# Vector engine's order set in the source for a gated-attention and MLP kernel: additions, low parts, and bank evacuations by twos

## The chip, the core and the metric

The kernel runs on one core of one Trainium2 chip. The time is the device time of one execution in microseconds (us), the median of three runs.

## The reference

One layer of a streaming encoder on 256 tokens of width 2048, in float32: a gated linear attention, then a squared-ReLU MLP, each on a normalized input and added to the residual, and a last normalization.

```python
h = h + _gla_mixer(_rmsnorm(h, gla_norm[j]), ...)
h = h + _sq_relu_mlp(_rmsnorm(h, mlp_norm[i]), mlp_w_up[i], mlp_w_down[i])
return _rmsnorm(h, final_norm)

def _sq_relu_mlp(h, w_up, w_down):
    a = jax.nn.relu(h @ w_up)
    return (a * a) @ w_down
```

`w_up` is 2048 x 8192 and `w_down` 8192 x 2048. The change touches only the MLP.

## The kernel before

**High and low parts.** Every float32 matrix is multiplied as two parts: `hi`, a cast to the matmul's own format (ScalarE), and `lo`, the rest `x - hi` (the Vector engine). A product is three matmuls, hi x hi, hi x lo and lo x hi. So each 512 KB piece of weights goes through four stations: a load on SyncE's queue into one of six `raw` tiles, a cast on ScalarE into one of five `hi` slots, a subtraction on the Vector engine into one of five `lo` slots, and the matmuls on TensorE. `parts` (lines 117 and 118) does cast and subtraction for the down weights, `weights` (L137, L138) for the up weights. A matmul here has a 128 x 128 stationary operand and 256 moving columns.

**The MLP.** The hidden width of 8192 is cut into eight rounds (`ROUNDS`) of 1024. For each round the generator `up` multiplies the tokens with a part of `w_up`, in two halves (`q`) of eight steps; a step (`turned_steps`, L186) has 24 matmuls and sums into two banks of PSUM. At certain steps (`even`, in most rounds the fourth) the weights stand in the slot with a gap between their two halves (`gap=`), which shifts the second half by 64 bytes. At the end of a half, `forms` reads the two banks (`su`, L687), squares (ScalarE, L691), makes sums and differences of the blocks (L695) and their hi and lo (L702, L703); these `act` tiles are the stationary operands of the down product.

The generator `down` runs over `passes`: for each round four groups `g` of 512 output columns, and in each group four steps `kp`. Up and down steps alternate: the main loop takes one up step after each `yield` of `down`, and `up` begins 18 steps ahead. The groups are walked forward in odd and backward in even rounds, so that the group at the turn keeps its banks.

**Sums.** For most steps (`by_sums`) the down product of a 2 x 2 block is done with seven block products in place of eight, on sums of blocks. Such a step has two parts: 9 matmuls on three of the raw blocks (`lo<-raw` of 768 columns), and 12 matmuls on four sums of the raw blocks. The sums are made by three additions on the Vector engine (L754) in one of two `work` halves, then cast and subtracted like other weights (`hi<-work`, `lo<-work`). The other steps have 24 matmuls on the raw blocks. In a round of the middle, 11 steps have sums and 5 have none.

**Ends of a group.** A group sums into four banks (`b16`, `b32`, `b57`, `bx4`). After its last step two of them are added to `sums` tiles (L775; the first time copied on ScalarE, L773) and two to the residual `h` (`take`, L709). The list `free` hands banks on in order.

**Order.** The program is written down step by step, and a scheduler sets the order of each engine's queue out of it from data dependences and its own estimate of times. `tc.issue_after(ins)` puts what is issued inside it behind `ins` on the engine of `ins`. `last_hi` and `last_lo` hold the newest cast and subtraction. Small pieces of other work wait in the list `side` and are issued by `pump` during up steps.

Of the kernel before, what the change touches and what calls it, by code (L numbers as in the profile page):

```python
# [46 lines left out]
G = 1024  # L47
GT = 512
# [11 lines left out]
OFF = 48  # L60
EVEN = (5, 6)
MR = 2 * GT
# [6 lines left out]
def tile_gla_mlp(ctx, tc, x, xt, cols, w_vg, w_in, w_gate, w_out, w_up, w_down, final_norm, out):  # L69
    nc = tc.nc  # L70

    const = ctx.enter_context(tc.tile_pool(name="const", bufs=1))
    big = ctx.enter_context(tc.tile_pool(name="big", bufs=2))
# [8 lines left out]
    def psum_bank(i, name="acc"):  # L82
        return psum.tile([P, 512], F32, tag=f"b{i}", name=name)
# [10 lines left out]
    side = deque()  # L94
# [10 lines left out]
            side.popleft()()  # L105


    last_load, last_hi, last_lo = [None], [None], [None]

    def slots():  # L110
        return [wpool.tile([P, SLOT], F32R, tag=i, name=i) for i in ("hi", "lo")]

    def parts(raw, n, to, pieces=None):

        hi, lo = to
        for s in (slice(*p) for p in pieces or [(0, n)]):
            last_hi[0] = nc.scalar.copy(hi[:, s], raw[:, s])  # L117
            last_lo[0] = nc.vector.tensor_tensor(lo[:, s], raw[:, s], hi[:, s].bitcast(F32), op=ALU.subtract)  # L118
        return hi, lo
# [4 lines left out]
    def weights(src, n, pieces=None, room=None, gap=None):  # L124


        to = room or slots()
        raw = raw_tile()
        loads, pieces = pieces or ([(0, n)], [(0, n)])
        for s in (slice(*p) for p in loads):  # L130
            dst = raw[:, s]
            if len(src.shape) == 3:
                dst = dst.rearrange("p (i c) -> p i c", i=2)
                last_load[0] = nc.sync.dma_start(out=dst, in_=src)
                between = SLOT - OFF - 2 * GT if gap else 0
                to = [a[:, OFF - between : OFF + 2 * GT + between].rearrange("p (i c) -> p i c", i=2)[:, :, between:] for a in to]
                last_hi[0] = nc.scalar.copy(to[0], dst)  # L137
                last_lo[0] = nc.vector.tensor_tensor(to[1], dst, to[0].bitcast(F32), op=ALU.subtract)  # L138
# [34 lines left out]
    def turned_steps(row, w, c0, even, acc, flip=0):  # L173

        for kp in range(KT // 2):
            wh, wl = weights(w[2 * kp * P : 2 * (kp + 1) * P, c0 : c0 + GT].rearrange("(i p) c -> p i c", p=P), 2 * GT, gap=kp in even)
            for i in range(2):
                kt = 2 * kp + i
                ah, al = row(kt)
                for j in range(GT // P):  # L180
                    s = slice(j * P, (j + 1) * P)
                    k = j % 2 ^ flip
                    o = acc[j // 2][:, k * T : (k + 1) * T]
                    for n, (u, m) in enumerate(((wh, ah), (wh, al), (wl, ah))):

                        nc.tensor.matmul(  # L186
                            o, u[:, i, s], m, start=kt == 0 and n == 0 and j % 2 == 0,
                            stop=kt == KT - 1 and n == 2, skip_group_check=True,
                        )
                if kt < KT - 1:  # L190
                    pump()
            yield
# [160 lines left out]
    acc = natural(plain_x, rows(w_vg, 0, WMAX), WMAX, cuts, ahead=input_tile)  # L353
# [255 lines left out]
    acc = natural(row_o, rows(w_out, 0), G, HALF)  # L609
# [55 lines left out]
    free = deque([*acc_free, *aux_free])  # L665

    def up():
        for m in range(ROUNDS):
            for q in range(MR // GT):
                first = m == q == 0  # L670
                taken = [free.popleft() for _ in range(2)]
                acc = [psum_bank(i, "up") for i in taken]
                even = (6,) if first else (0,) if m == 0 else (3,) if q == 0 else ()
# [3 lines left out]
                act = big.tile([P, 4 * G + 64], F32R, tag="BC"[q], name="act")[:, OFF:-16]  # L677
                acts[m][q] = act = act.rearrange("p (b i f s) -> p b i f s", b=2, i=2, f=8)
                for b in range(2):
                    forms(m, 2 * q + b, acc[b], act[:, b])  # L680
# [27 lines left out]
    def take(bank, t, lo, n):  # L708
        nc.vector.tensor_tensor(h[:, t, lo : lo + n], bank, h[:, t, lo : lo + n], op=ALU.add)  # L709
# [4 lines left out]

    def down(passes):

        for n, (m, g) in enumerate(passes):
            if not n or passes[n - 1][1] != g:
                taken = [free.popleft() for _ in range(4)]
                b16, b32, b57, bx4 = (psum_bank(i) for i in taken)  # L720
            ends = n + 1 == len(passes) or passes[n + 1][1] != g
            for kp in range(KP):
                last = ends and kp == KP - 1
                at = lambda f: stationary(m, kp, f)

                def product(bank, o, a, w, c):

                    for i, (x, y) in enumerate(((0, 0), (0, 1), (1, 0))):
                        halves(bank[:, o], a[x], w[y][:, c], bank.name not in used, last and i == 2)
# [6 lines left out]
                if not by_sums(m, g, kp):  # L736
                    w = parts(raw, 2 * GT, slots())
# [3 lines left out]
                    yield  # L741
                    continue
                w = parts(raw, 2 * GT, slots(), [(T, 2 * GT)])
                block = lambda i: slice(i * T, (i + 1) * T)
                product(b16, left, at(A11), w, block(1))
                product(b32, right, at(A12), w, block(3))
                product(b32, left, at(S4), w, block(2))
                yield

                wk = work[:, n_sums[0] % 2]  # L750
                n_sums[0] += 1
                u = wk.rearrange("p (f s) -> p f s", f=4)
                raw = raw.rearrange("p (f s) -> p f s", f=4)
                add = lambda o, x, y: nc.vector.tensor_tensor(o, x, y, op=ALU.add)  # L754
# [5 lines left out]
                product(b57, left, at(S1), wu, block(0))  # L760
                product(b57, right, at(S3), wu, block(1))
                product(b16, right, at(S2), wu, block(2))
                product(bx4, right, at(A22), wu, block(3))
            if ends:

                e = sums[g]
                for dst, b in ((e[:, 1:3], b16), (None, b32), (e[:, 0::3], b57), (None, bx4)):
                    if dst is None:
                        take(b, 0 if b is b32 else 1, g * GT, GT)
                        continue  # L770
                    b = b.rearrange("p (f s) -> p f s", f=2)
                    if g not in begun:
                        nc.scalar.copy(dst, b)  # L773
                    else:
                        nc.vector.tensor_tensor(dst, b, dst, op=ALU.add)  # L775
                free.extend(taken)
                begun.add(g)
                if m == ROUNDS - 1 or m == ROUNDS - 2 and g > 1:
                    side.extend(combine(g))

    def combine(g):

# [117 lines left out]
```

## Time and profile before

| | before |
|---|---|
| median of 3 runs (lowest, highest) | 1106.53 us (1105.65, 1106.56) |
| the profiled execution | 1106.95 us, of which the span in the profile is 1104.9 us |
| TensorE clock granted | 0.998 of full speed over the span |
| load of a piece of `w_up`, `w_down`, issue to landing | 4.5 us, 4.0 us |
| read from and written to HBM | 206.92 MB, 2.10 MB |

PE is TensorE's matmuls, PEld its weight loads, DVE the Vector engine, ACT ScalarE, SP SyncE's queue. The end of a matmul is modelled at about 279 ns after its start, while the next one starts some 115 ns after it; so TensorE counts as busy over small gaps, and the number of matmuls in a stretch says more than its busy time. In rows of groups and waits, `<-` names what the engine stood idle for, in us.

### The profile page before, as it was taken

To read this page: it belongs to the slowest core of one execution; us is meant where nothing else is said; L and a number is where in the kernel's file an instruction comes from. 1 tells how busy PE (TensorE), PEld (TensorE's weight loads), DVE (VectorE), ACT (ScalarE), POOL (GpSimd) and SP (SyncE) were. 2 spreads that over 40 slices of the span, in tenths; PEclk is the share of its full clock that TensorE was granted. 3 is DMA by queue.
4 is the path that set the end of the run, shared out by engine and by line. 5 is a ranking of instruction groups with operands and counts; after the bars stand their busy time and mean duration, and the time that the engine had idled before them with its cause. 6 is when DMAs were issued, how large, how long until landed. Compare 5 with 4: busy or idle time off the path is not lost.

```text
span 1104.9 us, 22086 instructions
## 1 busy us (share of the span) xinstructions
PE 1083.0 (98%) x9202; PEld 1074.5 (97%) x9202; DVE 836.9 (76%) x1144; ACT 573.9 (52%) x723; POOL 12.8 (1%) x39
## 2 busy tenths in 40 slices
PE   9999999999999999999999999999999999999997
PEld 9999999999999999999999989999999999999997
DVE  5777655555646567788798888898888889888887
ACT  6775445454535454565554444644545545544553
POOL 0000000100000000000000000000000000000000
PEclk9999999999999999999999999999999999999999
DMA  9857665556565654665666646665556666575672
GB/s 341 319 155 214 204 193 149 156 159 187 190 189 175 191 175 151 187 211 175 191 190 185 198 154 203 186 212 169 184 177 194 192 184 194 170 226 172 201 238 77
DMA packets 94788, 210.45 MB, mean 190 GB/s; under 512 B 6704, under 2 KB 7600, under 8 KB 94560
## 3 DMA queue, kind: packets, MB, share of 16 engines
q1 hardware_dynamic: 93728, 206.99, 60.8%
q10 hardware_dynamic: 960, 2.05, 0.5%
q8 instruction: 72, 1.18, 0.4%
q14 instruction: 28, 0.23, 0.1%
HBM read 206.92 MB, written 2.10 MB: 189 GB/s over the span
## 4 chain that ended last, share of the span: by engine, by line
PE 86%; DVE 7%; issue 2%; ACT 2%; DMA 1%; SPq 0%; ACTq 0%; POOLq 0%; DVEq 0%; POOL 0%
PE acc L149 49%; PE up L186 28%; PE acc L186 6%; PE aux L186 2%; DVE lo L118 2%; ACT hi L117 1%; DVE lo L138 1%; DVE work L754 1%; DVE su L687 1%; DMA raw<-in_w_vg 1%; PE aux L149 1%; DMA zz<-in_xt 1%; PE aux L555 1%; PE aux L483 1%; DVE work L695 0%
## 5 line engine op out<-in xcount | busy, mean ns | idle before, releaser
L149 PE MATMUL acc<-hi,act 128*128 128x256 f32 x1864 | 336.7, 280 | 8.3 <-ACT hi L117 8.0
L118 DVE TENSOR_TENSOR lo<-raw,hi 128x768 fp32r<-128x768 f32 (+3 forms) x226 | 251.1, 1113 | 105.6 <-ACT hi L117 105.0
L149 PEld LDWEIGHTS acc<-hi,act 128*128 128x128 f32 x1864 | 277.7, 188 | 13.8 <-ACT hi L117 13.8
L117 ACT CAST hi<-raw 128x768 fp32r<-128x768 f32 (+3 forms) x226 | 216.3, 960 | 126.4 <-PE acc L149 103.0
L186 PE MATMUL up<-hl,hi 128*128 128x256 f32 x1024 | 281.7, 279 | 0.0
L186 PE MATMUL up<-hh,hi 128*128 128x256 f32 x1024 | 281.3, 279 | 0.0
L186 PE MATMUL up<-hh,lo 128*128 128x256 f32 x1024 | 273.1, 279 | 0.0
L149 PE MATMUL acc<-lo,act 128*128 128x256 f32 x932 | 221.3, 281 | 4.4 <-DVE lo L118 4.1
L138 DVE TENSOR_TENSOR lo<-raw,hi 128x1024 fp32r<-128x1024 f32 x160 | 194.9, 1219 | 36.9 <-ACT hi L137 36.0
L117 ACT CAST hi<-work 128x1024 fp32r<-128x1024 f32 x76 | 79.8, 1050 | 241.8 <-DVE work L754 230.6
L137 ACT CAST hi<-raw 128x1024 fp32r<-128x1024 f32 x160 | 167.3, 1046 | 62.9 <-PE acc L149 21.4
L186 PEld LDWEIGHTS up<-hl,hi 128*128 128x128 f32 x1024 | 192.2, 188 | 0.0
L186 PEld LDWEIGHTS up<-hh,hi 128*128 128x128 f32 x1024 | 192.2, 188 | 0.0
L186 PEld LDWEIGHTS up<-hh,lo 128*128 128x128 f32 x1024 | 186.8, 188 | 0.4
L149 PEld LDWEIGHTS acc<-lo,act 128*128 128x128 f32 x932 | 161.2, 188 | 6.4 <-DVE lo L118 6.3
L118 DVE TENSOR_TENSOR lo<-work,hi 128x1024 fp32r<-128x1024 f32 x76 | 93.0, 1224 | 69.0 <-ACT hi L117 69.0
L149 PE MATMUL acc<-hi,xA 128*128 128x256 f32 (+1 forms) x736 | 104.7, 280 | 0.1
L149 PEld LDWEIGHTS acc<-hi,xA 128*128 128x128 f32 x736 | 93.9, 189 | 0.3 <-ACT hi L117 0.3
L754 DVE TENSOR_TENSOR work<-work,raw 128x256 f32<-128x256 f32 x152 | 64.0, 421 | 2.8
L149 PE MATMUL acc<-lo,xA 128*128 128x256 f32 (+1 forms) x368 | 58.5, 279 | 0.1
L754 DVE TENSOR_TENSOR work<-raw 128x512 f32<-128x512 f32 x76 | 52.0, 684 | 0.0
L149 PEld LDWEIGHTS acc<-lo,xA 128*128 128x128 f32 x368 | 49.6, 188 | 0.3 <-DVE lo L118 0.3
(151 smaller groups left out, 1095.7 us busy)
## 6 DMA issues: line engine op xcount, KB each, us to landing
raw<-in_w_up SPq DMA_DIRECT2D x128, 512.0 KB, 4.5
raw<-in_w_down SPq DMA_DIRECT2D x128, 512.0 KB, 4.0
raw<-in_w_in SPq DMA_DIRECT2D x80, 512.0 KB, 3.8
raw<-in_w_out SPq DMA_DIRECT2D x32, 512.0 KB, 3.7
raw<-in_w_vg SPq DMA_DIRECT2D x14, 520.0 KB, 8.7
h<-in_x SPq DMA_DIRECT2D x4, 512.0 KB, 8.6
zz<-in_xt SPq DMA_DIRECT2D x3, 384.0 KB, 8.7
fb<-in_final_norm ACTq DMA_DIRECT2D x1, 1024.0 KB, 5.0
```

The lines of the kernel that those rows point to most:

```text
L117: last_hi[0] = nc.scalar.copy(hi[:, s], raw[:, s])
L118: last_lo[0] = nc.vector.tensor_tensor(lo[:, s], raw[:, s], hi[:, s].bitcast(F32), op=ALU.subtract)
L137: last_hi[0] = nc.scalar.copy(to[0], dst)
L138: last_lo[0] = nc.vector.tensor_tensor(to[1], dst, to[0].bitcast(F32), op=ALU.subtract)
L149: nc.tensor.matmul(o[:, m], x, w[:, m], start=first and c == 0, stop=last, skip_group_check=True)
L186: nc.tensor.matmul(o, u[:, i, s], m, start=kt == 0 and n == 0 and j % 2 == 0, stop=kt == KT - 1 and n == 2, skip_group_check=True,)
L483: nc.tensor.matmul(o, kab[:, k[0], c0 + c, k[1] : k[1] + P], q(qt[:, c0 + c]), start=c == 0, stop=c == 1)
L555: nc.tensor.transpose(b[:, o + t * P : o + (t + 1) * P], src[:, t, kt * P : (kt + 1) * P], ident)
L687: nc.vector.scalar_tensor_tensor(s, bank.rearrange("p (i t) -> p i t", i=2), 0.0, r2row.unsqueeze(1).to_broadcast([P, 2, T]), op0=ALU.max, ...
L754: add = lambda o, x, y: nc.vector.tensor_tensor(o, x, y, op=ALU.add)
```

## The change

The source sets more of the Vector engine's order, and moves work to other steps:

- In `down`, the three additions are issued right behind the low part of their own step, ahead of the `yield`; a new `last_sum` holds the last of them, and the next up step's low part (in `weights`) is put behind it. The cast and low part of the sums come after the `yield`, behind that up step's low part.
- The four evacuations of a group are put in a list `late` and issued by `settle`, two at a time, after the up step of the next two steps.
- A group takes its banks in two pairs: `b16`, `b32` at its start, `b57`, `bx4` after the first `settle`.
- In `up`, the end of a half (the reading of its banks and the forms) is issued inside the next half's first step, behind that step's low part. Whatever is left is issued at the end.

Cut to its core:

```diff
     def up():
+        ended = []
...
-                yield from turned_steps(lambda kt: (hth[:, kt], htl[:, kt]), w_up, m * MR + q * GT, even, acc, 1)
+                for _ in turned_steps(lambda kt: (hth[:, kt], htl[:, kt]), w_up, m * MR + q * GT, even, acc, 1):
+
+                    while ended:
+                        with tc.issue_after(last_lo[0].ins):
+                            ended.pop(0)()
+                    yield
...
+                ended.append(end)
+        ended.pop()()
...
-                last_lo[0] = nc.vector.tensor_tensor(to[1], dst, to[0].bitcast(F32), op=ALU.subtract)
+                with ExitStack() as order:
+                    if last_sum[0]:
+                        order.enter_context(tc.issue_after(last_sum[0]))
+                    last_lo[0] = nc.vector.tensor_tensor(to[1], dst, to[0].bitcast(F32), op=ALU.subtract)
...
+        def settle(n=2):
+
+            with tc.issue_after(last_lo[0].ins):
+                for f in late[:n]:
+                    f()
+            del late[:n]
...
-                taken = [free.popleft() for _ in range(4)]
-                b16, b32, b57, bx4 = (psum_bank(i) for i in taken)
+                taken = [free.popleft() for _ in range(2)]
+                b16, b32 = (psum_bank(i) for i in taken)
+                b57 = None
...
+                    with tc.issue_after(last_lo[0].ins):
+                        add(u[:, :2], raw[:, :1].to_broadcast([P, 2, T]), raw[:, 1:3])
+                        add(u[:, 2], u[:, 0], raw[:, 2])
+                        last_sum[0] = add(u[:, 3], u[:, 2], raw[:, 3]).ins
...
                 yield
...
-                with tc.issue_after(last_lo[0].ins):
-                    add(u[:, :2], raw[:, :1].to_broadcast([P, 2, T]), raw[:, 1:3])
-                    add(u[:, 2], u[:, 0], raw[:, 2])
-                    add(u[:, 3], u[:, 2], raw[:, 3])
-                wu = parts(wk, G, slots())
+                settle()
+                if by_parts:
+                    if b57 is None:
+                        taken += [free.popleft() for _ in range(2)]
+                        b57, bx4 = (psum_bank(i) for i in taken[2:])
+
+                    with tc.issue_after(last_lo[0].ins):
+                        wu = parts(wk, G, slots())
...
-                free.extend(taken)
+                late.extend(lambda f=f, i=i: (f(), free.append(i)) for f, i in zip(fs, taken))
...
+        settle(len(late))
```

More of the change, by code (lines that the diff above doesn't have):

```diff
@@ L105, in flush @@
             side.popleft()()
-    last_load, last_hi, last_lo = [None], [None], [None]
+    last_load, last_hi, last_lo, last_sum = [None], [None], [None], [None]
     def slots():
@@ L667, in up, with end @@
     def up():
+        ended = []
         for m in range(ROUNDS):
             for q in range(MR // GT):
-                first = m == q == 0
                 taken = [free.popleft() for _ in range(2)]
                 acc = [psum_bank(i, "up") for i in taken]
-                even = (6,) if first else (0,) if m == 0 else (3,) if q == 0 else ()
-                yield from turned_steps(lambda kt: (hth[:, kt], htl[:, kt]), w_up, m * MR + q * GT, even, acc, 1)
+                even = (6,) if m == q == 0 else (0,) if m == 0 else (3,) if q == 0 else ()
+                for _ in turned_steps(lambda kt: (hth[:, kt], htl[:, kt]), w_up, m * MR + q * GT, even, acc, 1):
[3 more added lines that the diff above has]
+                    yield
                 if m == 0:
                     flush()
[L677 to L680, printed above, removed]
-                free.extend(taken)
+                def end(m=m, q=q, acc=acc, taken=taken):
+                    act = big.tile([P, 4 * G + 64], F32R, tag="BC"[q], name="act")[:, OFF:-16]
+                    acts[m][q] = act = act.rearrange("p (b i f s) -> p b i f s", b=2, i=2, f=8)
+                    for b in range(2):
+                        forms(m, 2 * q + b, acc[b], act[:, b])
+                    free.extend(taken)
+                ended.append(end)
+        ended.pop()()
     def forms(m, kp, bank, act):
@@ L715, in down @@
     def down(passes):
+        late = []
+        def settle(n=2):
[3 more added lines that the diff above has]
+            del late[:n]
         for n, (m, g) in enumerate(passes):
             if not n or passes[n - 1][1] != g:
-                taken = [free.popleft() for _ in range(4)]
-                b16, b32, b57, bx4 = (psum_bank(i) for i in taken)
+                taken = [free.popleft() for _ in range(2)]
+                b16, b32 = (psum_bank(i) for i in taken)
+                b57 = None
             ends = n + 1 == len(passes) or passes[n + 1][1] != g
@@ L735, in down @@
                 last_load[0] = nc.sync.dma_start(out=raw.rearrange("p (i c) -> p i c", i=2), in_=src)
-                if not by_sums(m, g, kp):
-                    w = parts(raw, 2 * GT, slots())
+                by_parts = by_sums(m, g, kp)
+                w = parts(raw, 2 * GT, slots(), [(T * by_parts, 2 * GT)])
+                if by_parts:
+                    block = lambda i: slice(i * T, (i + 1) * T)
+                    product(b16, left, at(A11), w, block(1))
+                    product(b32, right, at(A12), w, block(3))
+                    product(b32, left, at(S4), w, block(2))
+                    wk = work[:, n_sums[0] % 2]
+                    n_sums[0] += 1
+                    u = wk.rearrange("p (f s) -> p f s", f=4)
+                    raw = raw.rearrange("p (f s) -> p f s", f=4)
+                    add = lambda o, x, y: nc.vector.tensor_tensor(o, x, y, op=ALU.add)
+                    with tc.issue_after(last_lo[0].ins):
+                        add(u[:, :2], raw[:, :1].to_broadcast([P, 2, T]), raw[:, 1:3])
+                        add(u[:, 2], u[:, 0], raw[:, 2])
+                        last_sum[0] = add(u[:, 3], u[:, 2], raw[:, 3]).ins
+                else:
                     for i in range(2):
@@ L740, in down @@
                             product(bank, slice(0, GT), at(f[i]), w, slice(i * GT, (i + 1) * GT))
[L741 to L747, printed above, removed]
-                yield
-                wk = work[:, n_sums[0] % 2]
@@ L760, in down @@
[L760 to L763, printed above, removed]
+                yield
+                settle()
+                if by_parts:
+                    if b57 is None:
[3 more added lines that the diff above has]
+                        wu = parts(wk, G, slots())
+                    product(b57, left, at(S1), wu, block(0))
+                    product(b57, right, at(S3), wu, block(1))
+                    product(b16, right, at(S2), wu, block(2))
+                    product(bx4, right, at(A22), wu, block(3))
@@ L764, in down, with keep @@
             if ends:
                 e = sums[g]
[L767 to L770, printed above, removed]
+                def keep(dst, b, first=g not in begun):
                     b = b.rearrange("p (f s) -> p f s", f=2)
-                    if g not in begun:
+                    if first:
                         nc.scalar.copy(dst, b)
@@ L775, in down @@
                         nc.vector.tensor_tensor(dst, b, dst, op=ALU.add)
-                free.extend(taken)
                 begun.add(g)
+                fs = (
+                    lambda keep=keep, b=b16, e=e: keep(e[:, 1:3], b),
+                    lambda b=b32, g=g: take(b, 0, g * GT, GT),
+                    lambda keep=keep, b=b57, e=e: keep(e[:, 0::3], b),
+                    lambda b=bx4, g=g: take(b, 1, g * GT, GT),
+                )
+                late.extend(lambda f=f, i=i: (f(), free.append(i)) for f, i in zip(fs, taken))
                 if m == ROUNDS - 1 or m == ROUNDS - 2 and g > 1:
-                    side.extend(combine(g))
+                    late.append(lambda g=g: side.extend(combine(g)))
+        settle(len(late))
     def combine(g):
```

4 lines of the change are left out of this document (removed).

## The prediction

> **What bounds the kernel now.** I read first the page's busy table, then the windows cut at the MLP's rounds and in 20 us slices, the waits and line groups of the MLP stretch, the chain of waits, and the timeline of the Vector engine.
>
> ```profile
> PE 1083.0 (98%) x9202; PEld 1074.5 (97%) x9202; DVE 836.9 (76%) x1144; ACT 573.9 (52%) x723; POOL 12.8 (1%) x39
> ```
>
> By this row TensorE has 22 us of idle time and nothing else could be gained. The windows say otherwise: the MLP's interleaved stretch, two rounds of it, its tail, then slices (columns: span; busy us and count of PE, PEld, DVE, ACT, POOL; clock, DMA share, GB/s).
>
> ```profile
> 432.92:1042.37 609.45, 596.77 (x5016) 588.80 (x5014) 521.77 (x705) 309.45 (x353) 0.00 (x0) 1.00 0.61 188
> ...
> 609.99:701.50 91.51, 89.09 (x738) 87.21 (x737) 77.56 (x105) 45.92 (x52) 0.00 (x0) 1.00 0.61 187
> 701.50:790.60 89.10, 87.30 (x738) 86.20 (x736) 77.60 (x105) 44.62 (x52) 0.00 (x0) 1.00 0.62 188
> 1042.37:1096.66 54.29, 54.29 (x463) 54.29 (x462) 48.67 (x72) 28.27 (x42) 0.55 (x1) 1.00 0.45 148
> ...
> 980.00:1000.00 20.00, 20.00 (x179) 20.00 (x178) 17.04 (x23) 8.99 (x11) 0.00 (x0) 1.00 0.67 210
> 1000.00:1020.00 20.00, 20.00 (x179) 20.00 (x179) 19.17 (x30) 8.99 (x11) 0.00 (x0) 1.00 0.52 162
> 1020.00:1040.00 20.00, 19.36 (x162) 18.94 (x161) 17.45 (x24) 9.36 (x10) 0.00 (x0) 1.00 0.68 209
> 1040.00:1060.00 20.00, 20.00 (x172) 20.00 (x171) 17.72 (x24) 12.24 (x14) 0.00 (x0) 1.00 0.71 237
> ...
> 974.72 2.47 PE acc L149 x21
> 977.19 2.84 PE up L186 x24
> ...
> 984.57 2.27 PE up L186 x20
> 986.83 2.72 PE acc L149 x24
> ```
>
> The same 128x256 matmul runs at two spacings. The chain pieces (start, length, what) give 2.47/21 = 117.6 ns up to 977 and 2.27/20 = 113.5 and 2.72/24 = 113.3 ns after 980, on both kinds of line. Between them lies the 24 matmuls of U115, the fourth up step of its round, whose weights stand in the shifted layout (`gap`). Two slices with "20.00 busy" hold 179 matmuls; then comes a slice with 0.64 us idle, and the next busy slice holds 172. So a stall of TensorE costs twice: its own length, and 4.4 ns on each later matmul until the next shifted step, at most a round later. Clock 1.00 stands in every row, so the throttle isn't it.
>
> A round is 16 down steps and 16 up steps: eleven steps of 9+24+12 = 45 matmuls and five of 48, 735 in all, or 83.3 us at 113.3 ns. The two rounds took 91.51 and 89.10. From 432.92 (U18) to 1042.37 (U127) there are six rounds and 603 matmuls more, 5,013, or 568.0 us for the 609.45 taken; the 461 from 1042.37 take 54.29 for 52.2. **So 41.4 + 2.1 = 43.5 us are lost in the MLP to stalls and the slow spacing.**
>
> ```profile
> ACT hi L117 <- DVE work L754: 227.5, 64, 6.0
> PEld acc L149 <- ACT hi L117: 13.8, 28, 1.1
> PEld acc L149 <- DVE lo L118: 6.3, 9, 0.9
> ...
> L118 DVE TENSOR_TENSOR lo<-work,hi 128x1024 fp32r<-128x1024 f32 x73 | 89.4, 1224 | 67.2 <-ACT hi L117 67.2
> L754 DVE TENSOR_TENSOR work<-work,raw 128x256 f32<-128x256 f32 x146 | 61.5, 421 | 2.7
> L754 DVE TENSOR_TENSOR work<-raw 128x512 f32<-128x512 f32 x73 | 49.9, 684 | 0.0
> ```
>
> These are waits and groups of the stretch 432 to 1043. All TensorE stalls (the weight loader's 13.8 + 6.3 = 20.1 us; the other 23 us are spacing) are on the down product's hi and lo. They come late because of the Vector engine: its additions (L754) hold up ScalarE's cast of the sums, and then it stands 67.2 us, 0.92 in each of 73 steps, for that cast. With 77.6 busy and 11 x 0.92 = 10.1 waiting, Vector fills 87.7 of a round's 89 to 91 us. Its queue bounds the MLP; TensorE only looks full.
>
> **The change, part by part.** No instruction is added or removed: the built programs hold the same of each kind on each engine. Vector's queue goes, for a step n with sums (D = lo of the down weights, S = of the sums, U = of the up weights, evac = bank evacuations):
>
> ```
> before: S(n-1)  D(n)  U  add1 [evac, evac] add2 add3  (waits for the cast)  S(n)
> after:  S(n-1)  D(n)  add1 add2 add3  U  [evac] S(n) [evac]
> ```
>
> *The wait for the cast.* U now stands between add3 and S(n). It lasts 1.22 us; the cast that must fit under it is the 1.05 us of ScalarE below. So nearly all 0.92 us a step go, 10.1 us a round. That makes Vector 77.6 us a round against TensorE's 83.3, and TensorE the bound, if Vector's lead outlasts the bursts.
>
> *U moved behind the additions.* U is ready later by the additions, 0.68 + 2 x 0.42 = 1.5 us. The cover is the lead: hi and lo have five slots each, so Vector works up to four tiles ahead, where each tile is 1.02 (9 matmuls), 1.36 (12) or 2.72 us (24) of TensorE.
>
> *Evacuations and the forms of the up half, by twos and a step late.* They are the bursts; I price them by start-to-start distances of a stretch in which Vector never waited:
>
> ```profile
> 647.84 1.22 DVE L118 TENSOR_TENSOR lo<-raw,hi 128x1024 fp32r<-128x1024 f32 x1
> 648.98 1.22 DVE L138 TENSOR_TENSOR lo<-raw,hi 128x1024 fp32r<-128x1024 f32 x1
> 650.11 1.28 DVE L775 TENSOR_TENSOR sums<-acc,sums 128x512 f32<-128x512 f32 x2
> 651.31 0.95 DVE L118 TENSOR_TENSOR lo<-raw,hi 128x768 fp32r<-128x768 f32 x1
> 652.18 1.08 DVE L703 TENSOR_TENSOR act<-work,act 128x896 fp32r<-128x896 f32 x1
> 653.18 1.22 DVE L138 TENSOR_TENSOR lo<-raw,hi 128x1024 fp32r<-128x1024 f32 x1
> 654.31 0.68 DVE L754 TENSOR_TENSOR work<-raw 128x512 f32<-128x512 f32 x1
> 654.92 1.28 DVE L709 TENSOR_TENSOR h<-acc,h 128x512 f32<-128x512 f32 x2
> 656.12 0.41 DVE L695 TENSOR_TENSOR work<-work 128x256 f32<-128x256 f32 x1
> 656.45 0.41 DVE L754 TENSOR_TENSOR work<-work,raw 128x256 f32<-128x256 f32 x1
> 656.78 0.28 DVE L695 TENSOR_TENSOR work<-work 128x128 f32<-128x128 f32 x1
> 656.99 0.41 DVE L754 TENSOR_TENSOR work<-work,raw 128x256 f32<-128x256 f32 x1
> 657.32 0.28 DVE L695 TENSOR_TENSOR work<-work 128x128 f32<-128x128 f32 x1
> ...
> 645.62 1.05 ACT L117 CAST hi<-work 128x1024 fp32r<-128x1024 f32 x1 [4.29 <-DVE work L754]
> ```
>
> That is 1.13 for S, U and a D of 1024; 0.87 for a D of 768; 0.60 for an evacuation (and su, taken as equal: both read 512 from a bank); 1.00 for the act's lo; 0.61 for add1; 0.33 for add2, add3 and the wide L695; 0.21 for the narrow L695. The heaviest stretch is the middle of an even round. Time 0 is TensorE's end of U55, which frees su. TensorE then has S37, D38, U56 ready and needs S38 at 5.10, D39 at 6.46, U57 at 9.18, D40 at 11.90, U58 at 12.92, S40 at 15.64, D41 at 17.00, U59 at 18.02, S41 at 20.74. Vector, in the new order: su 0, S38 0.60, su 1.73, D39 2.33, L695 3.46, U57 3.79, D40 4.92, additions with two L695 5.79, U58 7.48, evac 8.61, act 9.21, evac 10.21, S40 10.81, D41 11.94, additions with two L695 12.81, U59 14.62 (done 15.84), evac, L695, evac 15.75, S41 17.16 (done 18.38). **The least lead is 2.2 us, before U59**; the two following steps without sums (2.3 us of Vector for 5.44) refill it. Two evacuations of 0.60 more in such a step would still fit; the cover is gone if Vector loses 2.2 us more in two steps.
>
> *Banks.* The next group's last two banks are now the old group's first two, so its first S product waits for the old b16 and b32. In Vector's queue these evacuations stand beside that step's S: at most one comes behind it, 0.6 us, inside the lead.
>
> *Other queues.* ScalarE now finds its cast of the sums ready after add3 and keeps its order otherwise; its 46 us of a 91 us round leave room. A load on SP waits for Vector to release a raw tile six tiles back, three steps or about 15 us, against 4.0 us to land:
>
> ```profile
> raw<-in_w_down SPq DMA_DIRECT2D x128, 512.0 KB, 4.0
> ```
>
> TensorE's own order becomes whole blocks (D 9, U 24, S 12), the same matmuls, so nothing there.
>
> *Sum.* If the stalls go, the fast spacing, reached in the up stage ahead of the MLP, is never lost: 43.5 us off. The profiled execution took 1106.95 us (span 1104.9 and 2.05 around it), the median 1106.53. 1106.95 - 43.5 = 1063.5; six shifted steps take 2.84 for 2.72 even so, 0.7, of which the spacing before paid most; I add 0.5: **1064.0 us**.
>
> The Trainium skill speaks against this: "TensorE: Matmul & The Clock Gate", section "Back-to-back issue gap", makes the warm gap of a lone matmul depend on its width alone, 262 cycles or 109 ns at 256. By that rule no stall could change the spacing, and only the waits would come back. The trace disagrees with its two spacings, 113.3 and 117.6.
>
> **The rivals.**
> *Only the waits return* (spacing stays slow, since something other than stalls, for instance the new block order, throws it back). For it: the record shows the return to 113.3 only at shifted steps. Against: 980 to 1020 stays fast over D, U and S alike. 1106.95 - 20.1 = 1087. Chance 0.08.
>
> *Vector becomes the bound.* If Vector's instructions did not overlap, a round would be the sum of their durations: 11 x (1.22 + 0.95 + 1.22 + 1.52) = 54.0, 5 x 2.44 = 12.2, twelve evacuations 8.2 at 0.68, forms about 9.6 (four su of 0.68, three sets of L695 of 0.97, four act of about 1.0): 84 us, over TensorE's 83.3. Leads then drain at the bursts; with a third of the loader's waits left, 7 us, and half the slow spacing, 12 us, it is 1063.5 + 19 = 1083. For it: Vector is at 93% of a fast round. Against: 647.84 to 657.6 shows starts 0.09 before the end of the one before. Chance 0.22. The Trainium skill is on this side: "VectorE: DVE Perf Modes", section "The DRAIN you can't avoid", says the next operation starts only when the pipe is empty; the trace shows the overlap.
>
> *Slower: the bank readers stall the queue.* su and the evacuations wait for TensorE, and S, which TensorE needs next, stands behind them in the same queue. If Vector has no lead there, each of 14 half ends and 21 group ends makes TensorE wait for one bank reader, a cast and S, 0.60 + 1.05 + 1.22: 2.9 us, 100 in place of 20.1, or 1106.95 + 80 = 1187; with half the places 1137. It decides at a lead of zero, 2.2 us from my least. Chance 0.06.
>
> *No effect* (the order is set, but the slots bind): 1106. Against: ScalarE waits 227.5 us for additions, not for slots. Chance 0.02.
>
> **How the numbers follow.** Mine 0.62, the others 0.22, 0.08, 0.06, 0.02. 0.2% is 2.2 us, about what a measurement can tell from none. Faster by more than that 0.92, within it 0.02, slower 0.06. The range takes my case and the two partial gains: down to 1061, since my edges are known to about 2 us, and up to 1088.
>
> **What would show it.** Right: no idle before lo<-work on Vector; loader waits on L149 under 3 us; every 20 us slice from 440 to 1090 with about 179 matmuls; rounds of 83 to 84 us. Spacing wrong: no waits, yet slices of 172. Lead wrong: loader waits on L149 at U59 or S41 kind of steps. Slower: su or h on Vector waiting for PE with TensorE idle right behind.

## The result and the profile after

| | before | after |
|---|---|---|
| median (lowest, highest), four runs each | 1106.55 us (1105.65, 1106.99) | 1064.68 us (1064.43, 1064.77) |
| span of the profiled execution | 1104.9 us | 1062.8 us |
| ratio to before, with 95% interval | | 0.9622 [0.9606, 0.9639] |

The changed kernel takes 41.9 us less; 1064.0 was forecast. Where a time below belongs to an experiment, its ratio is to runs of the kernel before on the same chip. Comparisons of a kernel whose executions fall into two groups use the shorter ones, so for such a kernel every execution is given.

The busy table of the page after, then the windows cut at the same steps of the MLP as before: U18 to U127, the two middle rounds from U50, the tail from U127, and one slice of 20 us (span; busy us and count of PE, PEld, DVE, ACT, POOL; clock, DMA share, GB/s).

```profile
PE 1053.7 (99%) x9202; PEld 1053.0 (99%) x9202; DVE 842.3 (79%) x1144; ACT 590.2 (56%) x723; POOL 13.2 (1%) x39
```

```profile
433.59:1002.29 568.70, 568.70 (x5015) 568.70 (x5014) 527.28 (x703) 326.88 (x354) 0.00 (x0) 1.00 0.64 202
600.35:683.73 83.38, 83.38 (x737) 83.38 (x736) 78.14 (x105) 47.78 (x52) 0.00 (x0) 1.00 0.65 203
683.73:767.11 83.38, 83.38 (x737) 83.38 (x736) 78.63 (x105) 47.90 (x52) 0.00 (x0) 1.00 0.64 202
1002.29:1054.54 52.25, 52.25 (x464) 52.25 (x462) 46.97 (x73) 27.34 (x41) 0.93 (x1) 1.00 0.44 145
1020.00:1040.00 20.00, 20.00 (x179) 20.00 (x178) 18.36 (x25) 10.98 (x12) 0.00 (x0) 1.00 0.57 184
```

The busy share of TensorE moved by one point, 98 to 99%, while 4% of the time went. The counts say where. Both rounds take 83.38 us for 735 matmuls, 113.4 ns each; before they took 91.51 and 89.10. The interleaved stretch fell from 609.45 to 568.70 us (40.75 less), the tail from 54.29 to 52.25 (2.04 less): 42.8 us together, where the two spans differ by 42.1: all of the gain. The other 0.7 us lie ahead of this: U18 starts at 433.59, before at 432.92. Vector's busy time of a round stayed (77.6 before, 78.1 and 78.6 after).

The waits of the stretch 432 to 1003 after (us in total, times, longest), and its two groups of instructions around the cast of the sums:

```profile
ACT hi L137 <- PE up L189: 80.7, 52, 2.0
ACT hi L117 <- PE up L189: 54.3, 51, 1.6
ACT hi L117 <- PE acc L152: 34.6, 37, 1.8
ACT hi L137 <- PE acc L152: 33.0, 39, 1.9
ACT hi L117 <- DVE work L770: 26.0, 27, 1.9
```

```profile
L118 DVE TENSOR_TENSOR lo<-work,hi 128x1024 fp32r<-128x1024 f32 x73 | 88.9, 1218 | 6.1 <-ACT hi L117 5.5
L117 ACT CAST hi<-work 128x1024 fp32r<-128x1024 f32 x73 | 77.0, 1054 | 40.0 <-DVE work L770 26.0 <-PE up L189 10.0 <-PE acc L152 2.6
```

The lines have moved: L118 is unchanged; before's L138, L149, L186 and L754 are L141, L152, L189 and L770, and its L695, L709 and L775 are L708, L722 and L802. Vector's idle time for the cast of the sums fell from 67.2 us to 5.5. (It also waits 18.8 us on L118 for casts of the raw pieces, which themselves wait for slots.) ScalarE, which had waited 227.5 us for the additions, now waits 26.0 for them and 202.6 for TensorE to release slots: the five slots are full, and Vector and ScalarE run ahead as far as these allow. No wait of PE or PEld on the down product's hi or lo is left in the stretch; before there were 20.1 us.

I also took the distances from one matmul's start to the next from the records, 5,531 in the MLP from its 17th up step (U16) on, and sorted what each lasts over 113.3 ns: distances up to 119.5 ns count as the slow spacing, up to 127 as a shifted step, longer ones as stalls. Before: 4,124 slow distances cost 18.4 us, shifted steps 0.5, stalls 24.6. After: 11 distances at the slow spacing cost 0.04 us, shifted steps 0.5, stalls nothing. The experiments below use this count.

### The profile page after: what moved, and what is told of

Its sections match the earlier page's. It is cut to its first block, busy times and chain, and to the rows that moved or that the text cites. A ratio compares the mean times of both kernels' runs of the same rounds, so it can differ in the third digit from the quotient of the medians.

```text
span 1062.8 us, 22112 instructions
## 1 busy us (share of the span) xinstructions
PE 1053.7 (99%) x9202; PEld 1053.0 (99%) x9202; DVE 842.3 (79%) x1144; ACT 590.2 (56%) x723; POOL 13.2 (1%) x39
## 4 chain that ended last, share of the span: by engine, by line
PE 97%; DMA 2%; issue 0%; SPq 0%; DVE 0%; ACT 0%; POOL 0%; POOLq 0%; DVEq 0%; ACTq 0%
PE acc L152 53%; PE up L189 33%; PE acc L189 6%; PE aux L189 2%; DMA raw<-in_w_vg 1%; PE aux L152 1%; PE aux L558 1%; DMA zz<-in_xt 1%; PE aux L486 1%; SPq L144 0%; DVE lo L118 0%; ACT hi L117 0%; POOL rf L321 0%; PE acc L387 0%; SPq L278 0%
## 5 line engine op out<-in xcount | busy, mean ns | idle before, releaser
L118 DVE TENSOR_TENSOR lo<-raw,hi 128x768 fp32r<-128x768 f32 (+3 forms) x226 | 251.5, 1115 | 124.4 <-ACT hi L117 123.5
L152 PE MATMUL acc<-hi,act 128*128 128x256 f32 x1864 | 323.2, 276 | 0.0
L189 PE MATMUL up<-hl,hi 128*128 128x256 f32 x1024 | 282.9, 276 | 0.0
L189 PE MATMUL up<-hh,hi 128*128 128x256 f32 x1024 | 282.8, 277 | 0.0
L189 PE MATMUL up<-hh,lo 128*128 128x256 f32 x1024 | 282.5, 276 | 0.0
L152 PEld LDWEIGHTS acc<-hi,act 128*128 128x128 f32 x1864 | 274.7, 188 | 0.0
L137 ACT CAST hi<-raw 128x1024 fp32r<-128x1024 f32 x160 | 167.9, 1051 | 166.7 <-PE up L189 91.4
L141 DVE TENSOR_TENSOR lo<-raw,hi 128x1024 fp32r<-128x1024 f32 x160 | 195.2, 1222 | 46.2 <-ACT hi L137 39.6
L152 PE MATMUL acc<-lo,act 128*128 128x256 f32 x932 | 225.4, 276 | 0.0
L189 PEld LDWEIGHTS up<-hl,hi 128*128 128x128 f32 x1024 | 192.4, 188 | 0.0
L189 PEld LDWEIGHTS up<-hh,hi 128*128 128x128 f32 x1024 | 192.3, 188 | 0.0
L189 PEld LDWEIGHTS up<-hh,lo 128*128 128x128 f32 x1024 | 192.1, 188 | 0.0
L152 PEld LDWEIGHTS acc<-lo,act 128*128 128x128 f32 x932 | 160.6, 188 | 0.0
L152 PE MATMUL acc<-hi,xA 128*128 128x256 f32 (+1 forms) x736 | 105.3, 281 | 0.0
L118 DVE TENSOR_TENSOR lo<-work,hi 128x1024 fp32r<-128x1024 f32 x76 | 92.6, 1218 | 8.8 <-ACT hi L117 8.2
L152 PEld LDWEIGHTS acc<-hi,xA 128*128 128x128 f32 x736 | 94.4, 189 | 0.4 <-ACT hi L117 0.2
L770 DVE TENSOR_TENSOR work<-work,raw 128x256 f32<-128x256 f32 x152 | 64.2, 423 | 3.7
L152 PE MATMUL acc<-lo,xA 128*128 128x256 f32 (+1 forms) x368 | 58.6, 279 | 0.0
L770 DVE TENSOR_TENSOR work<-raw 128x512 f32<-128x512 f32 x76 | 51.9, 683 | 0.0
L152 PEld LDWEIGHTS acc<-lo,xA 128*128 128x128 f32 x368 | 49.8, 189 | 0.3 <-DVE lo L118 0.3
```

The costliest lines, as they stand in the source:

```text
L152: nc.tensor.matmul(o[:, m], x, w[:, m], start=first and c == 0, stop=last, skip_group_check=True)
L189: nc.tensor.matmul(o, u[:, i, s], m, start=kt == 0 and n == 0 and j % 2 == 0, stop=kt == KT - 1 and n == 2, skip_group_check=True,)
```

## The experiments

My theory: Vector's wait for the cast starves the slots, TensorE stalls, and each stall brings the slow spacing until a shifted step ends it. Three questions follow: which part of the change does it, whether the spacing behaves as I said, and how much lead there is.

### Which part of the change

**The order alone.** Before, with the additions ahead of the `yield`, the up step's low part behind them, and the sums' cast and low part behind that. Evacuations and half ends stay as before.

```diff
+                    if last_sum[0]:
+                        order.enter_context(tc.issue_after(last_sum[0]))
...
-                yield
...
-                    add(u[:, 3], u[:, 2], raw[:, 3])
-                wu = parts(wk, G, slots())
+                    last_sum[0] = add(u[:, 3], u[:, 2], raw[:, 3]).ins
+                yield
+                with tc.issue_after(last_lo[0].ins):
+                    wu = parts(wk, G, slots())
```

> The kernel before with the order part alone: the additions ahead of the yield, the next up step's low part behind them, the sums' low part behind that. Evacuations are all four at the end of the group, the ends of the up halves and the banks as before. If the wait for the cast was the cause, nearly all of the gain comes: no idle before lo<-work, loader waits of 0 to 5 us, 1064 to 1076 us. Rival, that the bursts of evacuations are the cause: the stalls at the group ends stay, 1090 us or more.

Measured: 1065.02 us (1064.82 to 1065.64), ratio 0.9624 [0.9608, 0.9640]. The group that had stood idle 67.2 us:

```profile
L118 DVE TENSOR_TENSOR lo<-work,hi 128x1024 fp32r<-128x1024 f32 x73 | 89.1, 1220 | 5.4 <-ACT hi L117 4.4
```

**The late evacuations alone.** After, with the additions behind the `yield` again and nothing tied to them or to the sums' parts.

```diff
-                        last_sum[0] = add(u[:, 3], u[:, 2], raw[:, 3]).ins
...
                 yield
+                if by_parts:
+                    with tc.issue_after(last_lo[0].ins):
+                        add(u[:, :2], raw[:, :1].to_broadcast([P, 2, T]), raw[:, 1:3])
...
-                    with tc.issue_after(last_lo[0].ins):
-                        wu = parts(wk, G, slots())
+                    wu = parts(wk, G, slots())
```

> The changed kernel without the order part: evacuations by twos a step late, banks in pairs and the late end of an up half stay, but the additions are issued after the yield, behind the up step's low part, as before. If the wait for the cast was the cause, Vector still stands 0.9 us in each of 73 steps, 87 us a round, and the time stays at 1092 to 1110 us. Rival, that the late evacuations are what helped: 1065 to 1080 us.

Measured: 1108.12 us (1104.97 to 1109.87, ten runs), ratio 1.0012 [1.0001, 1.0022]. Its group and its largest wait of the loader, 432 to 1040:

```profile
L118 DVE TENSOR_TENSOR lo<-work,hi 128x1024 fp32r<-128x1024 f32 x73 | 89.4, 1225 | 73.7 <-ACT hi L117 73.7
```

```profile
PEld acc L152 <- ACT hi L117: 19.3, 27, 1.8
```

**No halving.** After, with all four evacuations at once.

```diff
-        def settle(n=2):
+        def settle(n=4):
```

> The changed kernel with all four evacuations in the one step after the group, not two and two. By the running sum of the heaviest stretch this puts 1.2 us more into the first of two steps and takes it out of the second; the least lead stays about 2 us. So no stall and the same time, 1064.7 us within 1 us. Rival, that the halving is needed: a stall at each of about 20 group ends and slow spacing for part of each round, 1075 us or more.

Measured: 1064.87 us (1064.51 to 1065.16), 0.9621 [0.9607, 0.9635]. The three together: the order is the whole gain, within what these runs can tell. Without it, late ends and evacuations by twos bring nothing; with it, neither they nor their halving is measurable.

**Early additions, but no cover.** After, with the sums' cast and low part directly behind the additions, and the up step's low part behind them all. The additions are as early as in after; only what stands between add3 and the sums' low part is gone.

```diff
                         last_sum[0] = add(u[:, 3], u[:, 2], raw[:, 3]).ins
+                    wu = parts(wk, G, slots())
+                    last_sum[0] = last_lo[0].ins
...
-                    with tc.issue_after(last_lo[0].ins):
-                        wu = parts(wk, G, slots())
```

> The changed kernel with the sums' cast and low part ahead of the next up step's low part: the additions are as early as in the change, but nothing stands between them and the sums' low part, so Vector waits 0.9 us for the cast in each of 76 steps again, 87.7 us a round. If that wait was the cause: stalls and slow spacing, 1090 to 1108 us. Rival, that it is enough to have the additions early: 1065 to 1070 us.

Measured: 1099.39 us (1098.73 to 1101.02), 0.9947 [0.9929, 0.9965]. The group, 432 to 1030:

```profile
L118 DVE TENSOR_TENSOR lo<-work,hi 128x1024 fp32r<-128x1024 f32 x72 | 88.2, 1225 | 72.3 <-ACT hi L117 72.3
```

One us of idle time in each of 72 steps is back, and with it 34.7 of the 41.9 us. So it is the up step's low part over the cast that brings the gain, not that the additions come early. The run isn't before over again, though: its loader waits for the up product (9.8 us on `hi L137`), as neither before nor after does, and why 7 us of the gain stay isn't shown.

### The spacing

**No shifted step inside the MLP's rounds, and none at all.** After, with `even` cut twice:

```diff
-                even = (6,) if m == q == 0 else (0,) if m == 0 else (3,) if q == 0 else ()
+                even = (6,) if m == q == 0 else (0,) if m == 0 else ()
```

> The changed kernel without the shifted weight layout in every round after the first (the two shifted steps of the first round stay). If a stall is what makes the spacing of the matmuls slow, there is nothing to repair: 113.3 ns to the end, and some 0.1 us saved in each of seven shifted steps, 1064 us (1063 to 1065). Rival, that the spacing drifts back by itself and the shifted steps hold it: up to 1064.7 + 22 = 1087 us, with slices of 172 matmuls in 20 us from the first round on.

```diff
+                even = ()
```

> The changed kernel without any shifted layout in the up steps. If only a shifted step brings the fast spacing back, the matmuls from the seventh up step on, some 5,770, all run at 117.7 ns: 5,770 x 4.4 ns = 25 us more, 1090 us (1087 to 1091), and still no wait of TensorE. Rival, that the order of the queues brings the fast spacing: 1065 us.

Measured: 1064.18 us (1063.59 to 1065.19), 0.9616 [0.9601, 0.9630], and 1089.83 us (1089.45 to 1090.59), 0.9847 [0.9833, 0.9862]. The first has not one slow distance in 5,531 and the second nothing else, without a stall in either. The same slice of the first and of the second:

```profile
800.00:820.00 20.00, 20.00 (x179) 20.00 (x178) 20.00 (x29) 12.11 (x13) 0.00 (x0) 1.00 0.64 199
...
800.00:820.00 20.00, 20.00 (x172) 20.00 (x171) 18.96 (x28) 11.54 (x13) 0.00 (x0) 1.00 0.61 185
```

Both spacings hold by themselves for hundreds of us, over down and up products alike, and the two shifted steps ahead of U18 choose the one. Undisturbed, the later shifted steps aren't needed. The second kernel has two shifted steps fewer and is 25.65 us longer than the first. The Trainium skill ("TensorE: Matmul & The Clock Gate", "Back-to-back issue gap") gives a lone matmul one warm gap for each width, 262 cycles at 256, and says that in a stream of weight loads and matmuls both together set the spacing, with one figure for each of the widths 128 and 512. These two runs are such a stream at 256, and one figure doesn't hold for it: clock 1.00 in both, 113.3 ns in the one and 117.7 in the other.

**More shifted steps in before.** If the slow spacing cost before 18 us and a shifted step ended it, four to a half round should return a good part.

```diff
-                even = (6,) if first else (0,) if m == 0 else (3,) if q == 0 else ()
+                even = (6,) if first else (0,) if m == 0 else (1, 3, 5, 7)
```

> The kernel before, with the shifted layout in every other up step of all rounds after the first. If slow spacing were simply added to the waits, nearly all of its 18 to 23 us would go: 1086 to 1090 us. If Vector's queue bounds the rounds at about 87.7 us (77.6 busy and 10.1 waiting for the cast), a faster TensorE only waits longer: rounds stay at 87 to 90 us, the loader's waits grow over their 20 us, and the time is 1093 to 1102 us.

Measured: 1102.31 us (1102.03 to 1103.24), 0.9961 [0.9947, 0.9975], 0.3 us over the far end of what I expected. The slow distances fell from 18.4 us to 7.3, but the shifted steps cost 3.9 themselves, where before they cost 0.5, and the stalls grew from 24.6 to 27.0:

```profile
PEld acc L149 <- ACT hi L117: 15.3, 31, 1.0
PEld acc L149 <- DVE lo L118: 5.7, 9, 0.8
```

These are its loader's waits, 432 to 1040; in before they were 13.8 and 6.3. So of the 11.1 us less at the slow spacing, 3.4 went into the shifted steps, 2.4 into longer stalls, and 5.3 stayed. The five rounds from U34 on take 87.6 to 90.9 us, where I had worked out 87.7 for Vector's queue: that agrees with Vector as the bound. But the stalls took back only a fifth of what the spacing gave, so this run doesn't show it by itself.

**One stall.** The first kernel of this part (no shifted step in the rounds), with twelve more runs of add3 in one step ahead of U35.

```diff
+                        for _ in range(12 if n == 4 and kp == 1 else 0):
+                            last_sum[0] = add(u[:, 3], u[:, 2], raw[:, 3]).ins
```

> As x1 (no shifted layout after the first round), and the last addition of one step of the second round (D17) is done 12 more times, 5.5 us on Vector, once. If a stall sets the spacing: one stall of 1 to 3 us near 526 us, and every matmul after it, some 4,650, at 117.7 ns: 1064 + 2 + 20.5 = 1086 us (1082 to 1089). Rival, that stalls and spacing have nothing to do with each other: 1064 + 1 to 3 = 1066 us.

Measured: four executions, 1065.56, 1086.78, 1086.44 and 1066.30 us. The profiled one is the first. Its stall is in the waits of 440 to 1000, and its windows show what followed:

```profile
PE acc L152 <- ACT hi L117: 1.4, 1, 1.4
```

```profile
520.00:540.00 20.00, 18.56 (x164) 18.37 (x164) 19.48 (x28) 11.61 (x14) 0.00 (x0) 1.00 0.64 210
540.00:560.00 20.00, 20.00 (x179) 20.00 (x178) 19.08 (x28) 11.72 (x14) 0.00 (x0) 1.00 0.65 213
```

My theory wanted 1086 and its rival 1066; the same program gave both, twice each. The two long executions have no profile; their granted clock, 0.997 and 0.998, lies in the range of the short ones, 0.997 and 0.999, and their 20 to 21 us are what some 4,650 matmuls at 4.4 ns more come to. In the profiled execution the stall did not bring the slow spacing. What the others suggest, that a stall leaves open which spacing comes next, the next kernel's trace decides.

**Five stalls.** The same addition to the same kernel at five places, one in each of five rounds.

```diff
+                        for _ in range(12 if n in (4, 8, 12, 16, 20) and kp == 1 else 0):
```

> As x4, but with the 12 additions in the same step of five rounds in place of one, and no shifted step after the first round. x4 gave 1066 us in two executions and 1086.6 in two: a stall seems to draw the spacing anew, fast or slow, and it then stays. If so, the trace shows stretches of both spacings that change only at the five stalls, in both directions and without a shifted step, and the executions differ: 1064 + 5 x 1.7 + 0 to 21 = 1073 to 1094 us. Rival, that the first stall made the spacing slow and the slow runs of x4 had another cause: all executions near 1073 or all near 1094 us.

Measured: four executions, 1080.20, 1080.43, 1088.08 and 1085.91 us; ratio 0.9813 [0.9776, 0.9850]. In the profiled one (1080.20) the stalls begin at 521.6, 606.6, 694.9, 782.6 and 870.4. Slices between them:

```profile
540.00:560.00 20.00, 20.00 (x179) 20.00 (x178) 18.97 (x29) 11.71 (x14) 0.00 (x0) 1.00 0.67 212
...
620.00:640.00 20.00, 20.00 (x173) 20.00 (x172) 19.86 (x30) 11.35 (x13) 0.00 (x0) 1.00 0.65 212
720.00:740.00 20.00, 20.00 (x173) 20.00 (x172) 18.93 (x29) 11.55 (x13) 0.00 (x0) 1.00 0.61 190
820.00:840.00 20.00, 20.00 (x173) 20.00 (x172) 17.72 (x25) 10.89 (x12) 0.00 (x0) 1.00 0.67 211
920.00:940.00 20.00, 20.00 (x179) 20.00 (x178) 19.06 (x26) 11.37 (x13) 0.00 (x0) 1.00 0.69 210
```

By the counts, the first stall left the spacing fast, the second made it slow, the third and fourth left it slow, and the fifth made it fast, with no shifted step anywhere near. Together with the one stall, a stall goes both ways in both directions. What decides it, these runs don't tell.

### The lead

**Four slots.** After, with one slot fewer for hi and lo each.

```diff
-    wpool = ctx.enter_context(tc.tile_pool(name="wpool", bufs=5))
+    wpool = ctx.enter_context(tc.tile_pool(name="wpool", bufs=4))
```

> The changed kernel with four slots for hi and lo in place of five. Vector's lead before U is then bounded by three tiles, 5.1 us less the cast and the subtraction, 2.8 us, in place of 3.8. If the lead is what hides the bursts, it gives out in some of the heavy stretches: stalls of about 0.5 us once or twice a round and slow spacing after them, 1068 to 1085 us. Rival, that Vector's mean load alone decides: 1065 us.

Measured: 1067.71 us (1067.44 to 1068.08), 0.9647 [0.9633, 0.9661], a little under what I expected, and not by the mechanism I expected. No heavy stretch of a round stalls: the rounds are as long as in after. One of the two:

```profile
600.35:683.73 83.38, 83.38 (x737) 83.38 (x736) 77.75 (x106) 47.71 (x52) 0.00 (x0) 1.00 0.64 203
```

The MLP's distances grew by 1.1 us only (627.41 to 628.54), nearly all of it in the tail: a stall of 0.15 us at 1029.8 and, behind it, nearly all of 226 distances at the slow spacing. Of the other 2 us in the profiled execution, 0.7 lie ahead of U18 (434.27 against 433.59) and 1.4 behind the last of the counted matmuls. The lead did shrink: U44's low part is done at 569.84 and first read at 570.55, 0.7 us later, where after has 2.6 (567.11, 569.75). It did not reach zero in the rounds. The edit isn't the slots alone, though: TensorE's queue here takes the first four matmuls of U44, which read only the cast, ahead of 20 of the down product.

**Vector's work lengthened by less and by more than the lead.** After, with add3 repeated in a heavy step of each of the rounds 0, 2 and 4, three times in one kernel, eight in the other. A repeat took 0.44 us, so these are 1.3 and 3.5 us.

```diff
+                        for _ in range(3 if g == 1 and kp == 0 and m in (0, 2, 4) else 0):
+                            last_sum[0] = add(u[:, 3], u[:, 2], raw[:, 3]).ins
```

> The changed kernel with 1.3 us more on Vector in the heaviest step of the rounds 0, 2 and 4 (the last addition of group 1's first step done three more times, 0.45 us each). The running sum left a least lead of 2.2 us behind that step, so it should still fit: no stall, 1064.7 us within 1 us. Rival, that there is no such lead (TensorE follows Vector closely): a stall of 1 us in each of three rounds and some slow spacing after it, 1068 us or more.

```diff
+                        for _ in range(8 if g == 1 and kp == 1 and m in (0, 2, 4) else 0):
+                            last_sum[0] = add(u[:, 3], u[:, 2], raw[:, 3]).ins
```

> The changed kernel with 3.6 us more on Vector in the second step of group 1 in the rounds 0, 2 and 4 (eight more additions of 0.45 us). The least lead of 2.2 to 2.4 us is used up: one stall of some 1.3 us in each of three rounds, and after each, in some executions, slow spacing until the next shifted step, at most 370 matmuls or 1.6 us: 1064.7 + 4 to 9 = 1068 to 1074 us. Rival, that the lead is much longer than the running sum says: 1064.7 us.

Measured: 1064.38 us (1064.03 to 1064.59), 0.9628 [0.9612, 0.9643]: the 1.3 us cost nothing. The long one took 1079.02 us (1078.37 to 1084.07), 0.9770 [0.9744, 0.9797], 5 us over the end of what I expected. Its stalls came as foreseen, in 440 to 1000:

```profile
PE acc L152 <- ACT hi L117: 3.7, 3, 1.4
```

What was wrong is how long the slow spacing lasted. In the profiled execution (1084.07) the three stalls cost 4.5 us and 3,321 slow distances 14.9. Its chain of waits (start, length, what), at the first shifted step after a stall and at the next one:

```profile
522.64 2.47 PE acc L152 x21
525.11 2.86 PE up L189 x24
527.97 2.47 PE acc L152 x21
...
609.24 2.47 PE acc L152 x21
611.71 2.84 PE up L189 x24
614.55 2.38 PE acc L152 x21
616.93 2.72 PE up L189 x24
```

After U35 (525.11) 21 matmuls still take 2.47 us, 117.6 ns each; after the step at 611.71 they take 2.38, 113.3 each. After each of the three stalls the first shifted step failed and the next one worked. In all three pairs the two kinds differ a little in length, 2.86 and 2.84 us. Why, no run shows.

## Why the prediction was right, step by step

**What bounds the kernel: right, its split a little off.** The 43.5 us lost in the MLP were there and 42.9 of them went, by the count of slow distances, shifted steps and stalls. I had put 20.1 on stalls, by the loader's waits, and 23 on spacing. By distances it is 24.6 and 18.4: behind most stalls a second distance is lengthened too, to some 0.22 us, which the waits don't count. By this split the rival in which only the waits return would have stood at 1082 us and not 1087.

**The cast covered by the up step's low part: right, and shown** by three kernels: order alone 1065.02, late ends alone 1108.12, no cover 1099.39.

**The lead covers the bursts: right, the heaviest place wrong.** The timeline of the Vector engine after (start, length): U44's low part, then the stretch that I had laid out; behind it, TensorE's first matmul of U44 and of U59:

```profile
565.89 1.22 DVE L141 TENSOR_TENSOR lo<-raw,hi 128x1024 fp32r<-128x1024 f32 x1
...
639.34 1.21 DVE L118 TENSOR_TENSOR lo<-work,hi 128x1024 fp32r<-128x1024 f32 x1
640.47 0.95 DVE L118 TENSOR_TENSOR lo<-raw,hi 128x768 fp32r<-128x768 f32 x1
641.34 0.68 DVE L770 TENSOR_TENSOR work<-raw 128x512 f32<-128x512 f32 x1
641.94 0.42 DVE L708 TENSOR_TENSOR work<-work 128x256 f32<-128x256 f32 x1
642.28 0.41 DVE L770 TENSOR_TENSOR work<-work,raw 128x256 f32<-128x256 f32 x1
642.62 0.28 DVE L708 TENSOR_TENSOR work<-work 128x128 f32<-128x128 f32 x1
642.82 0.41 DVE L770 TENSOR_TENSOR work<-work,raw 128x256 f32<-128x256 f32 x1
643.15 1.22 DVE L141 TENSOR_TENSOR lo<-raw,hi 128x1024 fp32r<-128x1024 f32 x1
644.29 0.68 DVE L802 TENSOR_TENSOR sums<-acc,sums 128x512 f32<-128x512 f32 x1
```

```profile
569.07 0.28 PE L189 MATMUL up<-hh,hi 128*128 128x256 f32 x1
...
647.01 0.28 PE L189 MATMUL up<-hh,hi 128*128 128x256 f32 x1
```

D41, the three additions with two forms between, then U59 (643.15) as laid out. It is done at 644.37 and TensorE begins it at 647.01: a lead of 2.64 us, where I had 2.2. But it isn't the least. U44, in an odd round, is done at 567.11 and begun at 569.07, 1.96 us, and U76 and U108 have the same. (By the records of all steps S26, S58 and S90 are begun 1.13 us behind their low parts, since two of their matmuls are taken early; but these two read only the cast, and the first that reads the low part comes 3.6 us behind it. S118, in the tail, has 1.95.) I had laid out the heaviest stretch of even rounds only. The margin held; the place of its least was mistaken, and that the least came out near 2.2 is in part luck.

**Evacuations, half ends, banks: right at no cost, and no more.** Neither late ends nor twos move the time.

**"So a stall of TensorE costs twice: its own length, and 4.4 ns on each later matmul until the next shifted step, at most a round later": wrong in two ways.** A stall can leave the spacing fast (one stall, 1065.56 and 1066.30) or even make it fast (five stalls, after 870.4), and a shifted step can fail to end the slow one (long lead, U35). It cost the forecast nothing, as after has no stall to apply it to; it put the long lead's run at 1068 to 1074 instead of 1079.

**The sum: 1064.0 against 1064.68.** The added 0.5 us for shifted steps is the 0.53 that they cost after, though not as I had counted it: there are seven and not six, at 2.80 us and not 2.84. The MLP gave 42.8 us for the 43.0 of the sum; the 0.7 us by which U18 starts later make up the rest.

**The rivals.** Only the waits return (1087): ruled out; the new block order keeps the fast spacing by itself, without later shifted steps. Vector as the bound (1083): the rows above start 0.08 us before the end of the one before, so a round needs 78 us and not 84. The Trainium skill's section behind that rival ("VectorE: DVE Perf Modes", "The DRAIN you can't avoid") says that the next operation waits for an empty pipe, but adds that one which is not held starts earlier, which the prediction left out; these rows start earlier. Bank readers (1137 to 1187): at U59's step they run at 644.29 and later, behind it, with TensorE 2.6 us away; the least lead in the rounds to a matmul that reads the low part is 2.6 us (U44). No effect (1106): excluded by the result.

## What to carry to other kernels

When one engine makes an operand, a second converts it and the first must work on it again, put independent work of the first engine between its two turns: here 1.22 us of it over a 1.05 us cast, in each step with sums, returned 42 us. Judge a full engine by instructions per slice, not by its busy share: 172 and 179 matmuls in 20 us both read as 100% busy. Lay the queue out against the times at which the consumer needs each tile, but for all kinds of rounds, and check the least lead in the trace after.

## What the runs showed of the hardware

A stream of 128x256 matmuls with a weight load for each ran at either 113.3 or 117.7 ns apart, at a granted clock of 1.00, and kept either for hundreds of us: 1064.18 against 1089.83 us for kernels that differ only in whether two early up steps have the second half of their weight tile shifted by 64 bytes. A stall of one to two us leaves the choice open again: five in one trace left it fast, slow, slow, slow and fast, and one program with one stall took 1065.56 to 1086.78 us. What sets the choice stays open.
